# Feed-forward weight tiles in rings with a fourth raw tile, DVE work ordered behind the last emptying, attention steps shifted by one

## The chip, the cores and the metric

The kernel runs on one core of one Trainium2 chip. The metric is the device time of one execution in microseconds (us); the time of a kernel is the median of its runs. The engines are TensorE (PE, with its weight loads PEld), VectorE (DVE), ScalarE (ACT), GpSimd (POOL) and SyncE (SP, which here only issues DMAs).

## The reference

One layer of a streaming encoder on 256 frames of width 2048, in float32. Cut to what matters:

```python
def swiglu(h, w1, w3, w2):
    return (jax.nn.silu(h @ w1) * (h @ w3)) @ w2

x = x + 0.5 * swiglu(rmsnorm(x, ffn1_norm_g), ffn1_w1, ffn1_w3, ffn1_w2)      # inner width 5632
h = rmsnorm(x, mix_norm_g)
qa, ka, va, cq, ckv, k_rope, ga, gb = split(h @ w_in)
y_a = diff_attention_branch(qa, ka, va, ...)       # 8 heads, two softmaxes each, ALiBi
y_b = mla_branch(cq, ckv, k_rope, ...)             # 16 heads, low-rank q and kv, rotary part of 64
merged = sigmoid(ga) * (y_a @ w_branch_a) + sigmoid(gb) * (y_b @ w_branch_b)
x = x + merged @ w_out
x = x + 0.5 * swiglu(rmsnorm(x, ffn2_norm_g), ffn2_w1, ffn2_w3, ffn2_w2)
```

Both attentions read frame s from frame t where s // 64 <= t // 64.

## The kernel before

**Precision.** Every float32 operand is split into a high part (ACT, a cast to fp32r, L120) and a low part (DVE, source less high part, L121); `split` does both. A product is three matmuls: high x high, high x low, low x high.

**Stages in time.** First feed-forward (0 to about 731 us, tiles named f_u and f_d), projection c and differential attention (to about 1090), latent attention (MLA, to about 1460) with the gate and branch products ga and ba of the first branch worked in between, the second branch and w_out (gb, bb, wo, to about 1692), second feed-forward (to the end).

**Feed-forward.** `ffn` walks over 11 groups of 512 inner columns. A group is one `gemm2` (name f_u), which makes the w1 and the w3 half together by Strassen-like sums: its 8 pairs of k-blocks are of kind "S" (seven products, 21 matmuls of 512 columns) or "P" (eight products, 24 matmuls). After groups 2, 5, 8 and 10 two `gemm2` calls (f_d) multiply by w2. That makes 19 `gemm2` calls in each feed-forward. Each uses all accumulators q1 to q7 in PSUM.

For each pair `gemm2` takes a raw tile of 1 MB, which SP loads in two DMAs of 512 KB (L329, L330). For a P pair ACT casts it and DVE subtracts (f_u_hp, f_u_lp). For an S pair DVE first makes sums of the raw quarters (L334, L335, L336), then ACT and DVE split the raw tile (hs, ls) and the sums (hw, lw). After the last pair DVE empties the accumulators: L361 (q5), L370 (q2 and q3), L371 (q4). From the second group on the pairs come in the order UP, whose kinds are S P P S P S P P; so the pair with i = 0 and the one with i = 3 are S.

The result of an f_d product that is not the last is added to x in DRAM by an accumulating DMA from POOL's queue (x_mid, L438).

**Weight tiles.** `wtile` hands out tiles for raw, high and low parts ("raw", "wh", "wl"): it counts modulo 3 while the pool w7 is open (in the feed-forwards) and modulo 2 elsewhere; number 2 lies in w7, numbers 0 and 1 in wp, which is open for the whole kernel. A tile that is handed out again is written when its last reader is done.

**The order of instructions.** The program is written as a stream; a scheduler then fixes, before the run, the order of instructions on each engine and each DMA queue. Every engine runs its own list in order. It may place an instruction of a later tile ahead of one that stands earlier in the source.

**Attention steps.** `later` appends steps to a list, `pend`; each block of a `gemm` (two k-blocks, 12 matmuls) and each pair of a `gemm2` is followed by one step from it; `wait` is an empty step. For two heads of MLA the steps are: `turn(0)` (transposes of the queries, tiles mt, mr, tn, tr), `turn(1)` (of the keys), `weigh` for each head (scores ms, L583; softmax me, L800 to L804), `turn_p` (transposes mp of the weights, L176), `mix` (times v). In one turn of the loop 3 blocks of mq, 2 of mk and 8 of ga or ba run. `branch_out` puts the gate ga through a sigmoid on ACT (L732) after the 8 blocks of ga. The rotary part of the queries is made on POOL (`rotate`, L550 to L552) and doubled by a copy on ACT (L753) before its transposes (mr).

Of the kernel before, what the change touches and what calls it, by code (L numbers as in the profile page):

```python
# [23 lines left out]
F32 = mybir.dt.float32  # L24
# [3 lines left out]
ALU = mybir.AluOpType  # L28
AX = mybir.AxisListType

P = 128
# [22 lines left out]
NW = 512  # L54
KT = 4
# [18 lines left out]
def tile_block(ctx: ExitStack, tc: tile.TileContext, a, out: bass.AP):  # L74
    nc = tc.nc
# [2 lines left out]

    const = ctx.enter_context(tc.tile_pool(name="const", bufs=1))
    big = ctx.enter_context(tc.tile_pool(name="big", bufs=1))  # L80
    pools, turnover = {}, {}
    wp = ctx.enter_context(tc.tile_pool(name="wp", bufs=2))

    def wtile(tag, dt, name):

        i = turnover[tag] = (turnover.get(tag, -1) + 1) % (3 if "w7" in pools else 2)
        if i < 2:
            return wp.tile([P, KT, NW], dt, tag=f"{tag}{i}", bufs=1, name=name)
        return pools["w7"].tile([P, KT, NW], dt, tag=tag, bufs=1, name=name)

    def enter(stack, key, **kw):
        pools[key] = stack.enter_context(tc.tile_pool(name=key, **kw))
        return pools[key]
# [24 lines left out]

    def split(hi, lo, src):
        nc.scalar.copy(out=hi, in_=src)  # L120
        nc.vector.tensor_sub(out=lo, in0=src, in1=hi.bitcast(F32))  # L121

    def split_scaled(hi, lo, src, scale):

# [9 lines left out]
    def later(*steps):  # L134
        pend.extend(steps)
# [43 lines left out]
    def put_transposed(T, kb0, nb, t, src, gain, tmp_pool, name):  # L179

        tp = transposes(lambda i: src[:, i * P:(i + 1) * P], nb, f"tp_{name}")
        sl = slice(t * P, (t + 1) * P)
        f = tmp_pool.tile([P, 4, P], F32, tag="ptf", bufs=1, name=f"f_{name}")
        if gain is None:
            nc.vector.tensor_copy(out=f[:, :nb], in_=tp)
        else:
            nc.vector.tensor_tensor(out=f[:, :nb], in0=tp, in1=gain.unsqueeze(2).to_broadcast([P, nb, P]), op=ALU.mult)
        split(T[:, 0, kb0:kb0 + nb, sl], T[:, 1, kb0:kb0 + nb, sl], f[:, :nb])
# [70 lines left out]
             ("q2", 1, "s", 2), ("q3", 6, "s", 3), ("q4", 3, "w", 2))  # L259
    PLAIN = (("q5", 2, 0), ("q2", 0, 1), ("q3", 4, 0), ("q4", 2, 1))  # L260

    def pair_views(t, n, w):
        return [t[:, i * 2 * w:(i + 1) * 2 * w, :].rearrange("p (h s) k -> p h s k", h=2) for i in range(n)]

# [33 lines left out]
    def gemm2(wleft, wright, pairs, name, due=None, x=None):  # L298
# [13 lines left out]
        def passes(T, prods, in_turn):  # L312


            high = lambda o, s, bh, bl: [(o, T[:, 0, s], bh), (o, T[:, 1, s], bh)]
            low = lambda o, s, bh, bl: [(o, T[:, 0, s], bl)]
            todo = [m for p in prods for f in (high, low) for m in f(*p)] if in_turn else \
                [m for f in (high, low) for p in prods for m in f(*p)]
            for o, x, b in todo:
                left[o] -= 1  # L320
                nc.tensor.matmul(out=q[o], lhsT=x, rhs=b, start=o not in started, stop=left[o] == 0)  # L321
                started.add(o)

        for i in range(n):
            if i == due:
                flush()
            kind, T, k = pairs[i]
            raw = wtile("raw", F32, f"{name}_w")
            nc.sync.dma_start(out=raw[:, 0::3], in_=wright(k))  # L329
            nc.sync.dma_start(out=raw[:, 1:3], in_=wleft(k))  # L330
            h4 = lambda m: (wtile("wh", F32R, f"{name}_h{m}"), wtile("wl", F32R, f"{name}_l{m}"))
            if kind == "S":
                sm = pools["w7"].tile([P, 3, NW], F32, tag="sum", bufs=1, name=f"{name}_s")
                nc.vector.tensor_tensor(out=sm[:, 0:2], in0=raw[:, 0:1].to_broadcast([P, 2, NW]), in1=raw[:, 1::2], op=ALU.add)  # L334
                nc.vector.tensor_add(out=raw[:, 0], in0=sm[:, 0], in1=raw[:, 3])  # L335
                nc.vector.tensor_add(out=sm[:, 2], in0=raw[:, 0], in1=raw[:, 2])  # L336
                sh, sl = h4("s")
                split(sh, sl, raw)
                wh, wl = h4("w")
                split(wh[:, 0:3], wl[:, 0:3], sm)  # L340
                B = {"s": (sh, sl), "w": (wh, wl)}
                for part in (("sw",) if i == 0 else ("s", "w")):
                    passes(T, [(o, slot, B[b][0][:, u], B[b][1][:, u]) for o, slot, b, u in SEVEN if b in part], i == 0)
            else:
                ph, pl = h4("p")
                split(ph, pl, raw)
                units = [(o, slot + j, 1 + j if l else 3 * j) for o, slot, l in PLAIN for j in range(2)]
                passes(T, [(o, slot, ph[:, u], pl[:, u]) for o, slot, u in units], i in (0, n - 1))
            if i == lastS:
                nc.scalar.copy(out=e11, in_=q["q1"])  # L350
                nc.vector.tensor_add(out=e12, in0=q["q6"], in1=e11)
                nc.vector.tensor_add(out=e21, in0=q["q7"], in1=e12)
                if x is not None:
                    (x11, x12), (x21, x22) = ((x[:, t, 0:NW], x[:, t, NW:]) for t in range(NT))
                    nc.vector.tensor_add(out=x11, in0=x11, in1=e11)
                    nc.vector.tensor_add(out=x21, in0=x21, in1=e21)
                    nc.vector.tensor_sub(out=x22, in0=x22, in1=e21)
            if pend:
                pend.pop(0)()
        if x is None:  # L360
            nc.vector.tensor_tensor(out=ev[:, :, NW:], in0=q["q5"].unsqueeze(1).to_broadcast([P, 2, NW]),  # L361
                                    in1=ev.rearrange("p t n -> p (t n)")[:, NW:3 * NW].rearrange("p (a n) -> p a n", a=2),
                                    op=ALU.subtract)
# [4 lines left out]
            nc.vector.tensor_add(out=x12, in0=x12, in1=e12)  # L368
            x1 = x[:, 0]
        nc.vector.tensor_add(out=x1, in0=q23.rearrange("p a n -> p (a n)"), in1=x1)  # L370
        nc.vector.tensor_add(out=x21, in0=q["q4"], in1=x21)  # L371
        return ev


# [67 lines left out]


    f1 = ExitStack()
    enter(f1, "w7", bufs=1)
    enter(f1, "ev", bufs=1)
    enter(f1, "acc", bufs=1, space=bass.MemoryType.PSUM)
    pool = pools["pt"] = f1.enter_context(tc.tile_pool(name="f1", bufs=1))
# [37 lines left out]

    ffn(T, rstd, a["ffn1_w1"][0], a["ffn1_w3"][0], a["ffn1_w2"][0], "D", "C", pool, done1, "f1")
    f1.close()
    del pools["acc"], pools["w7"]
    mixps = ExitStack()  # L490
    enter(mixps, "ps", bufs=2, space=bass.MemoryType.PSUM)
    ptx = ExitStack()
# [10 lines left out]
    with ExitStack() as mixers:  # L503
# [244 lines left out]
        for g in range(MLA_H // 2):  # L748
            qr = mw.tile([P, NT, 2, 2, ROPE], F32, tag="qr", bufs=1, name=f"qr{g}")
            qs, rq = first[0] if g == 0 else q_out(g, q_job(g), qr.rearrange("p t h x e -> p (t h x e)"))  # L750
            for t in range(NT):
                rotate(qr[:, t, :, 0], qs[:, t, :, NOPE:QK_DIM], rtab[0][:, t], [qr[:, t, :, x] for x in range(2)])
            nc.scalar.copy(out=qr[:, :, :, 1], in_=qr[:, :, :, 0])  # L753
            qkT = []

            def turn(i, nope, rope, g=g, qkT=qkT):
# [65 lines left out]
                split(ybT[:, 0, h], ybT[:, 1, h], op[:, 0:S])  # L822

            both = lambda f: [partial(f, hh) for hh in range(2)]
            later(wait, wait, wait, partial(turn, 1, kn, lambda t, w, kh=kh: kh[:, t, w:w + 2]), *both(weigh), wait, *both(turn_p), *both(mix))

            if g + 1 < MLA_H // 2:
                branch_out(g + 1, branch_job(g + 1))
# [37 lines left out]


    with ExitStack() as f2:
        enter(f2, "w7", bufs=1)
        enter(f2, "ev", bufs=1)  # L870
        enter(f2, "acc", bufs=1, space=bass.MemoryType.PSUM)
        pool = pools["pt"] = f2.enter_context(tc.tile_pool(name="f2", bufs=1))

        def done2(x, t, c):
            cs = slice(c * NW, (c + 1) * NW)
            nc.sync.dma_start(out=out_v[:, t, cs], in_=x[:, t, cs])

        ffn(T, rstd, a["ffn2_w1"][0], a["ffn2_w3"][0], a["ffn2_w2"][0], "D", "A", pool, done2, "f2")
        flush()
# [22 lines left out]
```

## Time and profile before

| | us |
|---|---|
| median of 3 runs | 2414.17 (2413.78 to 2415.47) |
| the profiled execution | 2412.0 |
| its span in the profile | 2410.1 |
| PE busy | 2370.2 (98%) |
| DVE busy | 1907.7 (79%) |
| ACT busy | 1256.1 (52%) |
| POOL busy | 127.1 (5%) |

How to read it: PE is busy nearly all the time, but a matmul's end in the profile is modelled, so that matmuls overlap in it and short pauses do not show. The other engines' busy shares are averages over stages that differ. A line of a view of groups reads: source line, engine, operation, written tile <- read tiles, shapes, count | busy us, mean ns | idle us just before, and what ended it. A line of the waits reads: engine, tile and line that waited <- what it waited for: us in total, times, longest. A line of the timeline reads: start us, duration us, engine, line, operation, tiles, count, and in brackets the idle time before it and what ended it. A line of the windows reads: stretch and its length, busy us and instructions of PE, PEld, DVE, ACT and POOL, the clock granted to TensorE (1.00 is full), the busy share of the 16 DMA engines, GB/s. A line of the chain of waits reads: start us, us, engine, tile, line and count of what set the end. A line of the DMA issues reads: tiles, queue, operation, count, KB each, median us from issue to landing.

### The profile page before, as it was taken

What the parts mean: (1) busy time and instruction counts of PE and PEld (TensorE: products, weight loads), DVE (VectorE), ACT (ScalarE), POOL (GpSimd) and SP (SyncE); (2) the same over time, 40 slices, a digit from 0 to 9 for tenths busy, and PEclk for the clock granted to TensorE, in tenths of its full rate; (3) what the DMA queues carried; (4) which work ended last, traced back from release to release, by engine and by line L of the source; (5) the groups of instructions that cost most, each with busy time, mean ns of one, the idle gap of its engine ahead of it and who ended that gap; (6) DMA issues with size and microseconds to landing.
All of it is one profiled execution on the core that took longest, in us unless ns stands there. A gap on an engine that the chain in (4) does not pass through costs nothing.

```text
span 2410.1 us, 29185 instructions
## 1 busy us (share of the span) xinstructions
PE 2370.2 (98%) x10940; PEld 1963.6 (81%) x10940; DVE 1907.7 (79%) x2395; ACT 1256.1 (52%) x1338; POOL 127.1 (5%) x185
## 2 busy tenths in 40 slices
PE   8999999999999999999999999999999999999999
PEld 6788888788788888888888888888788888878777
DVE  8998997988996676767777775556899899789798
ACT  5654554554554455545655644444555455455453
POOL 2000000000000100001121210000000000000000
PEclk9999999999999999999999999999999999999999
DMA  7567667657665545555455456576566766756764
GB/s 263 191 194 235 201 212 205 212 192 210 236 213 181 192 159 175 165 170 173 156 168 171 160 172 208 192 233 208 193 202 209 231 207 192 225 194 203 216 226 158
DMA packets 241918, 476.11 MB, mean 198 GB/s; under 512 B 15156, under 2 KB 28528, under 8 KB 241520
## 3 DMA queue, kind: packets, MB, share of 16 engines
q1 hardware_dynamic: 233280, 446.30, 56.1%
q0 software_dynamic: 7216, 27.29, 5.0%
q8 instruction: 86, 1.41, 0.2%
q10 hardware_dynamic: 1280, 0.66, 0.1%
q14 instruction: 56, 0.46, 0.1%
HBM read 451.12 MB, written 23.07 MB: 197 GB/s over the span
## 4 chain that ended last, share of the span: by engine, by line
PE 82%; DVE 8%; DMA 6%; issue 2%; ACT 1%; SPq 0%; DVEq 0%; ACTq 0%
PE f_u_q L321 29%; PE f_d_q L321 15%; PE da L164 7%; DMA f_u_w<-in_ffn_w 5%; PE ba L164 4%; PE dav L164 4%; PE wo L164 4%; PE bb L164 4%; PE gb L164 3%; PE c L164 2%; PE ga L164 2%; PE mq L164 2%; PE mk L164 2%; DVE f_u_ls L121 2%; DVE f_u_lp L121 2%
## 5 line engine op out<-in xcount | busy, mean ns | idle before, releaser
L120 ACT CAST f_u_hp<-f_u_w 128x2048 fp32r<-128x2048 f32 x110 | 210.1, 1912 | 177.1 <-PE f_u_q L321 101.5
L121 DVE TENSOR_TENSOR f_u_lp<-f_u_w,f_u_hp 128x2048 fp32r<-128x2048 f32 x110 | 250.9, 2285 | 3.7 <-ACT f_u_hp L120 3.7
L321 PE MATMUL f_d_q<-f_d_hp,f_gp 128*128 128x512 f32 x896 | 233.0, 391 | 0.0
L321 PE MATMUL f_u_q<-f_u_hp,hT1p 128*128 128x512 f32 x880 | 225.2, 393 | 0.6 <-ACT f_u_hp L120 0.5
L321 PE MATMUL f_u_q<-f_u_hp,hT2p 128*128 128x512 f32 x880 | 222.9, 390 | 0.2 <-ACT f_u_hp L120 0.2
L120 ACT CAST f_u_hs<-f_u_w 128x2048 fp32r<-128x2048 f32 x66 | 126.2, 1913 | 148.7 <-DVE f_u_w L335 109.4
L321 PEld LDWEIGHTS f_d_q<-f_d_hp,f_gp 128*128 128x128 f32 x896 | 167.3, 188 | 35.3 <-DVE f_gp L121 0.8
L321 PEld LDWEIGHTS f_u_q<-f_u_hp,hT1p 128*128 128x128 f32 x880 | 165.1, 189 | 35.7 <-ACT f_u_hp L120 1.4
L321 PEld LDWEIGHTS f_u_q<-f_u_hp,hT2p 128*128 128x128 f32 x880 | 164.6, 188 | 34.5 <-ACT f_u_hp L120 0.4
L121 DVE TENSOR_TENSOR f_u_ls<-f_u_w,f_u_hs 128x2048 fp32r<-128x2048 f32 x66 | 150.9, 2287 | 24.3 <-ACT f_u_hs L120 24.3
L120 ACT CAST f_d_hp<-f_d_w 128x2048 fp32r<-128x2048 f32 x60 | 113.9, 1913 | 106.2 <-PE f_d_q L321 43.9
L121 DVE TENSOR_TENSOR f_d_lp<-f_d_w,f_d_hp 128x2048 fp32r<-128x2048 f32 x60 | 136.3, 2287 | 23.6 <-ACT f_d_hp L120 23.6
L334 DVE TENSOR_TENSOR f_u_s<-f_u_w 128x1024 f32<-128x1024 f32 x66 | 80.7, 1223 | 72.1 <-DMA f_u_w<-in_ffn_w 72.1
L164 PE MATMUL da<-da_h,hTm 128*128 128x512 f32 x512 | 130.6, 396 | 0.0
L321 PE MATMUL f_d_q<-f_d_lp,f_gp 128*128 128x512 f32 x448 | 128.9, 389 | 0.0
L321 PE MATMUL f_u_q<-f_u_lp,hT2p 128*128 128x512 f32 x440 | 122.7, 391 | 2.1 <-DVE f_u_lp L121 2.0
L321 PE MATMUL f_u_q<-f_u_lp,hT1p 128*128 128x512 f32 x440 | 122.0, 390 | 0.0
L120 ACT CAST f_u_hw<-f_u_s 128x1536 fp32r<-128x1536 f32 x66 | 97.6, 1479 | 42.3 <-DVE f_u_s L336 29.9
L121 DVE TENSOR_TENSOR f_u_lw<-f_u_s,f_u_hw 128x1536 fp32r<-128x1536 f32 x66 | 115.6, 1751 | 0.0
L164 PEld LDWEIGHTS da<-da_h,hTm 128*128 128x128 f32 x512 | 93.4, 188 | 17.9
L321 PEld LDWEIGHTS f_u_q<-f_u_lp,hT2p 128*128 128x128 f32 x440 | 82.5, 188 | 21.0 <-DVE f_u_lp L121 4.0
L121 DVE TENSOR_TENSOR da_l<-da_w,da_h 128x1024 fp32r<-128x1024 f32 x64 | 76.8, 1220 | 28.1 <-ACT da_h L120 28.0
(381 smaller groups left out, 5009.0 us busy)
## 6 DMA issues: line engine op xcount, KB each, us to landing
f_u_w<-in_ffn_w SPq DMA_DIRECT2D x352, 512.0 KB, 4.7
f_d_w<-in_ffn_w SPq DMA_DIRECT2D x176, 512.0 KB, 5.1
da_w<-in_w_in SPq DMA_DIRECT2D x64, 512.0 KB, 4.5
dav_w<-in_w_in SPq DMA_DIRECT2D x32, 512.0 KB, 4.5
ga_w<-in_w_in SPq DMA_DIRECT2D x32, 512.0 KB, 4.6
ba_w<-in_w_branch_a SPq DMA_DIRECT2D x32, 512.0 KB, 4.9
gb_w<-in_w_in SPq DMA_DIRECT2D x32, 512.0 KB, 4.5
bb_w<-in_w_branch_b SPq DMA_DIRECT2D x32, 512.0 KB, 5.0
```

The lines of the kernel that those rows point to most:

```text
L120: nc.scalar.copy(out=hi, in_=src)
L121: nc.vector.tensor_sub(out=lo, in0=src, in1=hi.bitcast(F32))
L164: nc.tensor.matmul(out=po[t][:, :n], lhsT=l, rhs=r_, start=done[t] == 1, stop=done[t] == 3 * len(kbs))
L321: nc.tensor.matmul(out=q[o], lhsT=x, rhs=b, start=o not in started, stop=left[o] == 0)
L334: nc.vector.tensor_tensor(out=sm[:, 0:2], in0=raw[:, 0:1].to_broadcast([P, 2, NW]), in1=raw[:, 1::2], op=ALU.add)
```

## The change

Four things are changed.

1. `wtile` takes tiles from rings, one for each tag, the oldest first. In the feed-forwards the ring of raw tiles has four (two of wp and two of w7, three before), those of high and low parts three as before. `more_weights` adds the tiles of w7 behind the old ones, `fewer_weights` takes them out and keeps the order of the rest.
2. `split` returns its DVE instruction, and the last emptying of a `gemm2` (L371, q4) is noted in `emptied`. For every pair but the first of the next `gemm2`, the pair's first DVE instruction (L334 of an S pair, the low part of a P pair) is ordered behind it. It is an order on DVE's list, with no semaphore.
3. In MLA a `wait` stands ahead of the two `weigh` steps, and both are one step; the number of steps is the same. The copy of the rotary queries goes from ACT to POOL.
4. `put_transposed` uses the tile pf of `put_pairs` while the feed-forward's pools are open, in place of a tile of its own (ptf).

```diff
-    pools, turnover = {}, {}
+    pools = {}
+    rings = {tag: [0, 1] for tag in ("raw", "wh", "wl")}
...
     def wtile(tag, dt, name):
-        i = turnover[tag] = (turnover.get(tag, -1) + 1) % (3 if "w7" in pools else 2)
-        if i < 2:
-            return wp.tile([P, KT, NW], dt, tag=f"{tag}{i}", bufs=1, name=name)
-        return pools["w7"].tile([P, KT, NW], dt, tag=tag, bufs=1, name=name)
+        ring = rings[tag]
+        ring.append(ring.pop(0))
+        i = ring[-1]
+        return (wp if i < 2 else pools["w7"]).tile([P, KT, NW], dt, tag=f"{tag}{i}", bufs=1, name=name)
+
+    def more_weights(stack):
+        enter(stack, "w7", bufs=1)
+        for tag, new in (("raw", (2, 3)), ("wh", (2,)), ("wl", (2,))):
+            rings[tag].extend(new)
+
+    def fewer_weights():
+        del pools["w7"]
+        for ring in rings.values():
+            ring[:] = [i for i in ring if i < 2]
...
     def split(hi, lo, src):
         nc.scalar.copy(out=hi, in_=src)
-        nc.vector.tensor_sub(out=lo, in0=src, in1=hi.bitcast(F32))
+        return nc.vector.tensor_sub(out=lo, in0=src, in1=hi.bitcast(F32))
+
+    def behind(ins, first):
+        tc.add_manual_dep(ins.ins, first.ins.name, mybir.DependencyInfo(mybir.DependencyClass.NoSync, mybir.DependencyReason.DATA),
+                          reason="order")
...
-        f = tmp_pool.tile([P, 4, P], F32, tag="ptf", bufs=1, name=f"f_{name}")
+        if "acc" in pools:
+            f = tmp_pool.tile([P, 2, 7, P], F32, tag="pf", bufs=1, name=f"f_{name}").rearrange("p a s k -> p (a s) k")
+        else:
+            f = tmp_pool.tile([P, 4, P], F32, tag="ptf", bufs=1, name=f"f_{name}")
...
+    emptied = []
...
-                nc.vector.tensor_tensor(out=sm[:, 0:2], in0=raw[:, 0:1].to_broadcast([P, 2, NW]), in1=raw[:, 1::2], op=ALU.add)
+                early = nc.vector.tensor_tensor(out=sm[:, 0:2], in0=raw[:, 0:1].to_broadcast([P, 2, NW]), in1=raw[:, 1::2],
+                                                op=ALU.add)
...
-                split(ph, pl, raw)
+                early = split(ph, pl, raw)
...
+            if i and emptied:
+                behind(early, emptied[-1])
...
-        nc.vector.tensor_add(out=x21, in0=q["q4"], in1=x21)
+        emptied.append(nc.vector.tensor_add(out=x21, in0=q["q4"], in1=x21))
...
-    enter(f1, "w7", bufs=1)
+    more_weights(f1)
...
-    del pools["acc"], pools["w7"]
+    del pools["acc"]
+    fewer_weights()
...
-            nc.scalar.copy(out=qr[:, :, :, 1], in_=qr[:, :, :, 0])
+            nc.gpsimd.tensor_copy(out=qr[:, :, :, 1], in_=qr[:, :, :, 0])
...
-            later(wait, wait, wait, partial(turn, 1, kn, lambda t, w, kh=kh: kh[:, t, w:w + 2]), *both(weigh), wait, *both(turn_p), *both(mix))
+            later(wait, wait, wait, partial(turn, 1, kn, lambda t, w, kh=kh: kh[:, t, w:w + 2]), wait, lambda f=both(weigh): [s() for s in f],
+                  wait, *both(turn_p), *both(mix))
...
-        enter(f2, "w7", bufs=1)
+        more_weights(f2)
```

## The prediction

> **What bounds the kernel.** I read the page's busy times first, then the same by stage (the windows view), then who ended TensorE's idle time (the waits), then the timeline around the longest of those waits.
>
> ```profile
> PE 2370.2 (98%) x10940; PEld 1963.6 (81%) x10940; DVE 1907.7 (79%) x2395; ACT 1256.1 (52%) x1338; POOL 127.1 (5%) x185
> ...
> 1692.00:2405.00 713.00, 704.39 (x3123) 575.95 (x3123) 623.37 (x521) 373.95 (x271) 14.41 (x19) 1.00 0.65 206
> ```
>
> TensorE is the bound everywhere. In the second feed-forward (1692 to 2405) DVE is busy 623.37 of 713 us, 87%, and DMA 0.65: both are close behind. The change touches no matmul, so all that it can win is TensorE's idle time.
>
> A matmul row overstates that TensorE is busy:
>
> ```profile
> L321 PE MATMUL f_d_q<-f_d_hp,f_gp 128*128 128x512 f32 x896 | 233.0, 391 | 0.0
> ...
> 1838.59 47.87 PE f_d_q L321 x210
> ```
>
> A matmul lasts 391 ns, but in the chain 210 of them take 47.87 us, 228 ns apiece. So a wait that shows as x us of idle time costs x + 0.16 us. The waits, by stage: 75 to 731 us (first feed-forward without its filling), 731 to 760, 1090 to 1460, 1692 to 2405:
>
> ```profile
> PE f_u_q L321 <- DVE f_u_e L371: 2.9, 3, 1.2
> PE f_u_q L321 <- DVE f_u_lw L121: 1.0, 1, 1.0
> PE f_u_q L321 <- DVE f_d_e L371: 0.8, 1, 0.8
> ...
> PE c L164 <- DVE f_x L371: 1.9, 1, 1.9
> ...
> PE ms L583 <- DVE tn L126: 3.3, 4, 1.0
> ...
> PE ms L583 <- ACT tn L125: 0.8, 1, 0.8
> PE mp L176 <- DVE me L804: 0.6, 1, 0.6
> ...
> PE f_u_q L321 <- DVE f_u_e L371: 4.2, 4, 1.3
> PE f_u_q L321 <- DVE f_u_lp L121: 2.0, 4, 0.7
> ...
> PE f_u_q L321 <- DVE f_u_lw L121: 1.1, 1, 1.1
> PE f_u_q L321 <- ACT f_u_hs L120: 0.2, 1, 0.2
> PE f_u_q L321 <- ACT f_u_hp L120: 0.2, 1, 0.2
> ```
>
> **A, the order behind the last emptying.** At the end of a feed-forward product L371 empties the last accumulator (q4), and the next product cannot write that bank before. One of the eight L371 waits, on DVE and then on TensorE:
>
> ```profile
> 1928.64 1.23 DVE L370 TENSOR_TENSOR f_u_e<-f_u_q,f_u_e 128x1024 f32<-128x1024 f32 x1
> 1931.04 1.23 DVE L334 TENSOR_TENSOR f_u_s<-f_u_w 128x1024 f32<-128x1024 f32 x1 [1.17 <-DMA f_u_w<-in_ffn_w]
> 1932.18 0.69 DVE L371 TENSOR_TENSOR f_u_e<-f_u_q,f_u_e 128x512 f32<-128x512 f32 x1
> ...
> 1933.38 2.29 DVE L121 TENSOR_TENSOR f_u_lp<-f_u_w,f_u_hp 128x2048 fp32r<-128x2048 f32 x1
> ...
> 1932.92 0.73 PE L321 MATMUL f_u_q<-f_u_hw,hT2s 128*128 128x512 f32 x2 [0.91 <-DVE f_u_e L371]
> ...
> 1937.36 1.52 PE L321 MATMUL f_u_q<-f_u_lp,hT2p 128*128 128x512 f32 x6
> ```
>
> DVE runs in order. A weight sum of the next product (L334) stands ahead of L371 and waits 1.17 us for a load that has not landed, then takes 1.23 us; q4 is ready all that time. The sum belongs to the fourth pair in turn (i = 3), and the change puts the first DVE operation of every pair but the first behind L371. L371 then starts where L370 ends, 1929.87, and ends near 1930.6; TensorE came to need it at 1932.01 (1932.92 less 0.91). The wait goes with 1.4 us to spare. All eight have this shape in the timeline (L370, an idle L334, L371), so A is 2.9 + 0.8 + 4.2 = 7.9 us of idle time in 8 waits: 7.9 + 8 x 0.16 = **9.2 us**. It adds a wait inside DVE only; queued behind it are the sum and the low half f_u_lp, and TensorE waits for those next. Here f_u_lp ends at 1935.67 and its first use came at 1937.36; without the wait that use moves up by 0.91 + 0.16, to 1936.3, still later.
>
> **B, the fourth raw tile.** DVE's idle time ahead of sums, over the run, and the place where it hurts most:
>
> ```profile
> DVE f_u_s L334 <- DMA f_u_w<-in_ffn_w: 72.1, 40, 5.7
> ...
> 2234.52 0.37 SPq L329 DMA_DIRECT2D f_u_w<-in_ffn_w  x1
> ...
> 2245.02 1.23 DVE L334 TENSOR_TENSOR f_u_s<-f_u_w 128x1024 f32<-128x1024 f32 x1 [0.95 <-DMA f_u_w<-in_ffn_w]
> ...
> f_u_w<-in_ffn_w SPq DMA_DIRECT2D x352, 512.0 KB, 4.7
> ...
> x_mid<-f_d_e POOLq DMA_DIRECT2D x12, 1024.0 KB, 9.5
> ```
>
> SP issues a load when a raw tile comes free, and a usual load lands in 4.7 us. The one issued at 2234.52 held DVE until 2245.02, beside the accumulating store x_mid, which itself takes 9.5 us. With four tiles each load is issued one release earlier, here before that store begins. DVE's idle time (13% of this stage) moves ahead of the work, and the late f_u_lw and f_u_lp should go: lw 1.0 and 1.1, lp 2.0 less the 0.7 of term C, 3.4 us in 5 waits, 3.4 + 0.8 = 4.2 us. No row shows four tiles: at worst DVE does no earlier work that TensorE needs (0), at best all 4.2 go. I take half, **2.1 us**, since DVE at 87% stays the next bound and its order is rearranged.
>
> **C, rings.** Entering the second feed-forward, the tile that the old counter picks first is a new one, whose memory is the previous stage's:
>
> ```profile
> 1691.26 1.90 ACT L120 CAST f_u_hp<-f_u_w 128x2048 fp32r<-128x2048 f32 x1 [5.99 <-PE wo L164]
> ```
>
> The cast idles 5.99 us until the last wo product. In the ring the old tiles come first, oldest first, and the second raw load and this cast need not wait. Gone: lp 0.7, hs 0.2, hp 0.2, 1.1 + 3 x 0.16 = **1.6 us** (at worst 0). The 1.9 us wait of c is not touched: no product follows there, so no order is set. The first 75 us fill the pipeline from memory and DVE has no gap there: 0. The shared pf tile in place of ptf has one buffer as before, and its steps come after those of put_pairs: 0, and 0.7 (one 128x512 DVE operation) each for its four uses if they met.
>
> **D, attention steps.** The transposed keys (tn) are made by the step before the scores, with one block of 12 matmuls between:
>
> ```profile
> 1271.62 0.44 PE L583 MATMUL ms<-tn,tn 128*128 128x128 f32 x2 [0.77 <-DVE tn L126]
> ...
> 1276.49 1.28 ACT L732 ACT_TABLE_LOAD   x1
> 1277.79 1.27 ACT L732 ACTIVATE mg<-ga,rstd_n 128x512 f32<-128x512 f32 x2
> 1279.08 1.28 ACT L800 ACT_TABLE_LOAD   x1
> ...
> 1275.76 0.45 PE L583 MATMUL ms<-tn,tn 128*128 128x128 f32 x3
> ...
> 1277.07 4.23 PE mq L164 x24
> ...
> 1283.56 0.54 DVE L804 TENSOR_SCALAR me<-me,msm 128x128 f32<-128x128 f32 x2
> ```
>
> One more block, 12 x 0.228 = 2.7 us, lies between now, more than the longest wait (1.0): the five tn waits go, 3.3 + 0.8 + 5 x 0.16 = **4.9 us**. In exchange the first head's scores come 2.7 us later, just ahead of the second's. Both softmaxes then meet the gate's sigmoid with its table loads, 1.28 + 1.27 + 1.28 = 3.8 us of ACT, which only the second head met before. Late next is mp, the transposes of the weights. The one mp wait (0.6) bounds it: between 0 and 8 iterations x 0.76 = 6.1 us; I take half, **-3.0 us**.
>
> **E, the copy on POOL.** ACT's copy and POOL's nearest operations:
>
> ```profile
> L753 ACT COPY qr<-qr x8: 406/407/407, 1128.7 to 1414.1; 128x256 f32<-128x256 f32 x8
> L550 POOL TENSOR_TENSOR qr<-qs,rtab x32: 456/462/1311, 1125.0 to 1412.1; 128x128 f32<-128x128 f32 x32
> L176 PE MATMUL mr<-ident,qr x32: 272/273/273, 1134.1 to 1419.1; 128*128 128x128 f32 x32
> ```
>
> ACT no longer stands behind POOL's rotation, but TensorE waits for nothing of that. On POOL the copy has twice the elements of L550: between 0.46 and 2 x 1.31 = 2.6 us; I take 0.9. Its reader mr comes 5 us after the copy's start (1128.7 to 1134.1, 1414.1 to 1419.1), so even 2.6 is hidden: 0.
>
> **Sum:** 9.2 + 2.1 + 1.6 + 4.9 - 3.0 = 14.8 us. On the profiled execution, 2412.0 us (its span and 1.9 around it), that gives 2397.2; it ran 2.2 below the median of the three runs, 2414.17, so the forecast is 2414.17 - 14.8 = **2399.4 us**.
>
> **The clock** sets one more bound. After the wait of c:
>
> ```profile
> 728.08:731.49 3.41, 1.49 (x7) 0.96 (x7) 3.41 (x5) 2.82 (x7) 1.22 (x3) 1.00 0.66 162
> 731.49:734.90 3.41, 3.41 (x11) 3.02 (x10) 1.49 (x2) 1.40 (x4) 2.27 (x7) 0.50 1.02 360
> ```
>
> 1.9 us of idle time inside one 3.41 us stretch was followed by one at half clock, 3.41 x 0.5 = 1.7 us lost. If A and B move c against these stretches, the 1.7 may go. The Trainium skill (TensorE: Matmul & The Clock Gate, Part 1) asks for a whole idle window of about 3.4 us; by that rule 1.9 us would cost nothing, and the trace disagrees.
>
> **Rivals.**
>
> 1. *The loads share the engines.* The fourth load finds the 16 DMA engines taken and lands no earlier. For it: the load at 2234.52 next to x_mid. Against it: DMA is busy only 0.65. B and C bring nothing: 9.2 + 4.9 - 3.0 = 11.1, **2403.1**. The Trainium skill (DMA: Bandwidth & Descriptors, Issuing engines are not separate DMA queues) has a rule on this side: DMAs of all issuers run on the same 16 engines and interleave. The trace agrees at that one place.
> 2. *The scores meet the sigmoid.* Between the first head's scores and its mp lie the second head's scores (1275.76 to 1277.07, 1.3 us) and two blocks of mq (24 matmuls, 4.23 us). From the point where its softmax takes more than these 5.5 us, TensorE waits at mp. Before, the head that met the sigmoid took 7.0 us (scores done at 1277.07, weights at 1283.56 + 0.54): 1.5 + 0.16 = 1.7 us a time, 13.3 in 8 iterations. Then 9.2 + 2.1 + 1.6 + 4.9 - 13.3 = 4.5, **2409.7**. Against it: only every second iteration has a sigmoid.
> 3. *The stall moves, the change does not do what it says.* DVE's order is fixed beforehand. If other operations that wait for loads get ahead of urgent ones, the 72.1 us come back elsewhere: **2414**, no change.
> 4. *The order costs more than it frees.* DVE idles at each of the 36 ends of a product that have another after them, waiting for q4's last matmul, and f_u_lp comes late. Price 0.7 + 0.16 = 0.9 each (the longest lp wait), 31 us, less 14.8 won: **2430**. It decides from where f_u_lp slips by more than the 0.6 us left above (1935.67 to 1936.3). For it: DVE at 87%. Against it: its waits for loads give room.
>
> **Chances.** Forecast 0.57, own range 2392 (all of A to D without loss, 19.9, and the 1.7 of the clock) to 2405 (A alone); rival 1 0.13; rival 2 0.08; rival 3 0.12; rival 4 0.10. Differences under 0.2%, 4.8 us, cannot be told from no change. Faster is the forecast and rival 1, with a little of 2: 0.72; within 0.2% the rest of 2 and rival 3: 0.18; slower 0.10. From 2392 to 2413 lie the forecast, rivals 1 and 2 and the near half of 3, about 0.8.
>
> **What would show it.** Right: no TensorE wait on L371 in the feed-forwards; L334 behind L371 everywhere; f_u_lw and f_u_lp waits under 2 us; the cast at 1691 earlier; no ms wait on tn; mp waits of at most 0.8. Wrong: new TensorE waits on f_u_lp just after L371 (rival 4), mp waits of 1.5 us or more (rival 2), or loads still late beside x_mid (rival 1).

## The result, and the profile after

The changed kernel takes 2389.93 us (median, 2389.27 to 2392.05) and the kernel before, run beside it, 2414.82 us (2413.78 to 2416.05): a ratio of 0.9898, 95% interval 0.9881 to 0.9915. That is 24.9 us faster, where 14.8 were forecast, and 2.1 us below the lower end of the range. The direction was right; the size was too small. From profiled execution to profiled execution the difference is 2412.0 - 2389.9 = 22.1 us; the other 2.8 lie between the profiled run of before and its median.

The busy times of the changed kernel, and its second feed-forward in the windows view (columns: window, its length, then the busy time and instruction count of PE, PEld, DVE, ACT and POOL, granted clock, DMA share, GB/s):

```profile
PE 2359.4 (99%) x10940; PEld 1964.8 (82%) x10940; DVE 1913.0 (80%) x2395; ACT 1254.7 (53%) x1330; POOL 129.5 (5%) x193
...
1680.00:2383.00 703.00, 699.99 (x3127) 577.28 (x3125) 623.83 (x521) 373.79 (x270) 15.57 (x19) 1.00 0.65 209
```

TensorE's idle time in the second feed-forward fell from 713 - 704.4 = 8.6 us to 3.0. Here is what ended it, then the same for the start of c and for the latent attention (the waits view, by stage: total us, times, longest):

```profile
PE f_u_q L343 <- DVE x L886: 1.2, 1, 1.2
PE f_d_q L343 <- DVE f_gs L133: 0.8, 1, 0.8
PE f_u_q L343 <- DVE f_u_ls L133: 0.5, 1, 0.5
PE f_u_q L343 <- DVE f_u_lw L133: 0.4, 1, 0.4
...
PE c L181 <- ACT hTm L132: 2.2, 1, 2.2
PE c L181 <- DVE f_x L396: 1.9, 1, 1.9
...
PE mp L193 <- DVE me L830: 2.6, 5, 1.7
PE tp_ya L193 <- DVE f_ya L207: 0.7, 1, 0.7
```

Every wait of TensorE on the last emptying (L371 before, L396 now) is gone but that of c, which the change does not reach; so is every f_u_lp wait and every ms wait on tn. The mp waits have grown from one of 0.6 to five. DVE shows the other side, in the waits view of its own engine and in the timeline at the place that the prediction worked through (columns: start, length, engine, line):

```profile
DVE f_u_e L395 <- PE f_u_q L343: 17.9, 16, 1.1
DVE f_u_s L356 <- DMA f_u_w<-in_ffn_w: 12.4, 12, 1.8
...
1914.91 1.22 DVE L395 TENSOR_TENSOR f_u_e<-f_u_q,f_u_e 128x1024 f32<-128x1024 f32 x1 [1.12 <-PE f_u_q L343]
1916.27 0.69 DVE L396 TENSOR_TENSOR f_u_e<-f_u_q,f_u_e 128x512 f32<-128x512 f32 x1
1916.88 1.22 DVE L356 TENSOR_TENSOR f_u_s<-f_u_w 128x1024 f32<-128x1024 f32 x1
1918.01 2.29 DVE L133 TENSOR_TENSOR f_u_lp<-f_u_w,f_u_hp 128x2048 fp32r<-128x2048 f32 x1
```

DVE now stands for TensorE at the end of a product (17.9 us in 16 waits) and much less for the loads of f_u (72.1 us in 40 waits before, 12.4 in 12 now). For those of f_d it stands more (1.8 us in 2 waits before, 9.2 in 3 now). The sum L356 follows the last emptying at once and finds its load landed.

Where the 22.1 us came from, by the first matmul of each stage in the two traces (the filling up to tp_f; the first feed-forward up to c; c and the differential attention up to mq; the latent attention and both branches up to wo; wo and the second feed-forward):

| | filling | first FFN | c, diff. attention | latent attention | wo, second FFN |
|---|---|---|---|---|---|
| before | 73.9 | 657.2 | 358.6 | 510.5 | 809.9 |
| after | 75.3 | 650.9 | 357.9 | 505.5 | 798.4 |
| gain | -1.4 | 6.3 | 0.7 | 5.0 | 11.5 |
| forecast | 0 | 12.9 for both FFNs | 0 | 1.9 | |

The feed-forwards gave 17.8 instead of 12.9, the attention 5.0 instead of 1.9.

### The profile page after: what moved, and what is told of

Same layout as the page of the kernel before. It is cut to its first block, busy times and chain, and to the rows that moved or that the text cites. A ratio compares the mean times of both kernels' runs of the same rounds, so it can differ in the third digit from the quotient of the medians.

```text
span 2388.1 us, 29197 instructions
## 1 busy us (share of the span) xinstructions
PE 2359.4 (99%) x10940; PEld 1964.8 (82%) x10940; DVE 1913.0 (80%) x2395; ACT 1254.7 (53%) x1330; POOL 129.5 (5%) x193
## 4 chain that ended last, share of the span: by engine, by line
PE 92%; DVE 4%; DMA 2%; issue 1%; ACT 1%; SPq 0%; DVEq 0%; ACTq 0%
PE f_u_q L343 35%; PE f_d_q L343 18%; PE da L181 7%; PE dav L181 4%; PE ba L181 4%; PE wo L181 4%; PE ga L181 4%; PE bb L181 4%; PE gb L181 3%; PE c L181 2%; PE mk L181 2%; PE mq L181 1%; DMA f_d_w<-in_ffn_w 1%; PE tp_f L193 1%; PE ms L609 1%
## 5 line engine op out<-in xcount | busy, mean ns | idle before, releaser
L181 PEld LDWEIGHTS da<-da_h,hTm 128*128 128x128 f32 x512 | 93.4, 188 | 17.9
L343 PEld LDWEIGHTS f_d_q<-f_d_lp,f_gp 128*128 128x128 f32 x448 | 83.9, 188 | 18.5 <-DVE f_d_lp L133 1.1
L343 PEld LDWEIGHTS f_u_q<-f_u_lp,hT1p 128*128 128x128 f32 x440 | 83.1, 189 | 17.4
```

Of the source, the lines that this page charges most:

```text
L181: nc.tensor.matmul(out=po[t][:, :n], lhsT=l, rhs=r_, start=done[t] == 1, stop=done[t] == 3 * len(kbs))
```

## The experiments

These ran on three chips: e1 to e4, e13 and e14 on one, e5 to e8 on a second, e9 to e12 on a third. The kernel before takes 2409.36 us (median of 21 runs, 2406.72 to 2413.42) and 2409.23 on the first of them, 2408.89 on the second and 2409.86 on the third. The record does not name the chip of the result above, which is called the first set here. Each difference below is against the set that the run belongs to, and the stage lengths are cut as in the table above; each comes from one profiled execution.

**The order alone (e1_fence).** The kernel before with the order only:

```diff
-                split(ph, pl, raw)
+                early = split(ph, pl, raw)
...
+            if i and emptied:
+                behind(early, emptied[-1])
...
-        nc.vector.tensor_add(out=x21, in0=q["q4"], in1=x21)
+        emptied.append(nc.vector.tensor_add(out=x21, in0=q["q4"], in1=x21))
```

> Before, with only the order behind the last emptying added. Theory (the terms add, each with its own waits): the eight TensorE waits on L371 go and nothing else changes, 9.2 us less than before, 2405. Rival (the fence alone clears the DVE stall that makes later tiles late): the f_u_lp and f_u_lw waits go too, 13 us or more. Second rival (DVE idles at the fence): 5 us or less, with new waits on f_u_lp.

Measured: 2400.42 us, ratio 0.9966 (0.9953 to 0.9978), 8.9 us faster (5.3 to 11.3 by the interval). The feed-forwards' waits on the last emptying are gone, and no new f_u_lp wait has come. Term A, 9.2, lies inside the interval. The waits that were priced are not quite the same on these chips: the kernels below that keep the feed-forward of before (e3_mla, e8_shift, e14_copy) show six to eight of them, 6.2 to 7.0 us, which is 7.2 to 8.3 by the prediction's price.

**Rings and the fourth raw tile, without the order (e2_raw4).**

```diff
+        for tag, new in (("raw", (2, 3)), ("wh", (2,)), ("wl", (2,))):
+            rings[tag].extend(new)
```

> Before, with only the rings, the fourth raw tile and the shared pf tile. Theory (terms add): B whole and C, 5.8 us, and the pauses too short for the profile's idle time, about 3 us: 9 us less, 2406, with the L371 waits still there. Rival (the earlier loads also end the DVE idle time in front of L371): the L371 waits go without any fence, 15 us or more, and A and B are two ways to the same gain.

Measured: 2413.79 us, ratio 1.0021 (1.0011 to 1.003), 4.4 us slower, where the theory had 9 faster and its rival 15. The trace shows the place: in DVE's timeline, TensorE's timeline, then two windows of the columns above.

```profile
659.66 1.23 DVE L384 TENSOR_TENSOR f_u_e<-f_u_q,f_u_e 128x1024 f32<-128x1024 f32 x1 [1.11 <-PE f_u_q L335]
666.39 1.23 DVE L348 TENSOR_TENSOR f_d_s<-f_d_w 128x1024 f32<-128x1024 f32 x1 [5.51 <-DMA f_d_w<-in_ffn_w]
667.53 0.68 DVE L385 TENSOR_TENSOR f_u_e<-f_u_q,f_u_e 128x512 f32<-128x512 f32 x1
...
668.27 0.74 PE L335 MATMUL f_d_q<-f_d_hw,f_gp 128*128 128x512 f32 x2 [3.21 <-DVE f_u_e L385]
...
666.15:669.56 3.41, 1.29 (x6) 1.05 (x6) 3.17 (x4) 1.31 (x2) 0.00 (x0) 1.00 0.02 5
669.56:672.97 3.41, 3.41 (x10) 2.64 (x9) 3.41 (x5) 3.01 (x2) 0.00 (x0) 0.50 0.17 31
```

With four tiles DVE's order, fixed beforehand, has a sum of the next product (L348) ahead of the last emptying (L385); it stands 5.51 us for its load, and TensorE 3.21. The next 3.41 us run at a granted clock of 0.50. The old stall is longer at such places: two waits on L385 take 6.8 us, the longest 3.6, where the longest in the feed-forwards of before took 1.3. The trace has four half-clock stretches between the filling and the end, that of before one. Three more at 1.7 us apiece would be 5.1 us, an estimate about as large as the whole loss.

**The attention steps, with the copy on POOL (e3_mla) and without it (e8_shift).**

```diff
-            ...both(weigh), wait, *both(turn_p), *both(mix))
+            ...wait, lambda f=both(weigh): [s() for s in f],
+                  wait, *both(turn_p), *both(mix))
...
-            nc.scalar.copy(out=qr[:, :, :, 1], in_=qr[:, :, :, 0])
+            nc.gpsimd.tensor_copy(out=qr[:, :, :, 1], in_=qr[:, :, :, 0])
```

> Before, with only the shifted attention steps and the copy on POOL. Theory: the MLA stage gets shorter by 4.8 us as in the changed kernel, 2410. Rival (the stage gains only because the feed-forward change shifted its start and the clock stretches): 1 to 2 us.

> Before, with only the shift of the attention steps; the copy stays on ACT. Theory (the tn waits are the gain, and the clock that stays whole with them): all of the attention part, 7 to 9 us less than before. Rival (ACT, no longer stopped behind POOL's rotation, brings half): 3 to 5 us.

Measured: e3_mla 2400.97 us, ratio 0.9968 (0.9956 to 0.9981), 8.4 us faster; e8_shift 2403.27, ratio 0.9979 (0.9969 to 0.9989), 5.6 faster. The theory's 4.8 for e3_mla lies inside its interval (4.6 to 10.6); e8_shift falls between its theory (7 to 9) and its rival (3 to 5), and its interval (2.6 to 7.5) settles neither. The latent attention takes 504.9 us in the first and 506.2 in the second; it took 510.5 in the profile of before, and 510.6 to 512.6 in the six other traces with the old steps and the old copy. The tn waits are gone in both, and what is left in e3_mla are five mp waits and one of the stage's end:

```profile
PE mp L176 <- DVE me L804: 1.9, 5, 1.0
PE tp_ya L176 <- DVE f_ya L187: 0.8, 1, 0.8
```

**The copy alone (e14_copy).**

> The kernel before with the copy of the rotated queries on POOL alone, nothing else. The forecast's step E: 0, within 1.5 us of before, since its reader comes 5 us later. Rival: ACT's queue no longer stands behind POOL's rotation and short pauses of TensorE go: 1.5 to 3 us faster (the attention steps with the copy were 2.8 us ahead of the attention steps alone, at the edge of what those runs could tell).

Measured: 2406.08 us, ratio 0.999 (0.9981 to 0.9998), 3.1 us faster by the medians, 0.5 to 4.6 by the interval; the latent attention takes 508.0, 2.5 less than in the profile of before, and 2.6 to 4.6 less than in the six others. Step E had put this at 0, and the rival is nearer. The rows show what it missed: first e14's waits in the stage, then ACT's timeline in the kernel before, then in e14.

```profile
PE ms L583 <- DVE tn L126: 1.2, 2, 1.0
...
PE mp L176 <- DVE me L804: 0.6, 1, 0.6
```

```profile
1169.69 0.41 ACT L753 COPY qr<-qr 128x256 f32<-128x256 f32 x1 [4.59 <-DVE u_mq L114]
1170.00 1.04 ACT L120 CAST ga_h<-ga_w 128x1024 fp32r<-128x1024 f32 x1
...
1186.72 1.77 ACT L120 CAST mq_h<-mq_w 128x768 fp32r<-128x768 f32 x2 [5.48 <-DMA mq_w<-in_mla_w_qb]
1188.40 0.58 ACT L125 ACTIVATE tn<-mt 128x512 fp32r<-128x512 f32 x1
```

```profile
1169.11 1.05 ACT L120 CAST ga_h<-ga_w 128x1024 fp32r<-128x1024 f32 x1 [1.55 <-PE mk L164]
...
1188.45 1.78 ACT L120 CAST mq_h<-mq_w 128x768 fp32r<-128x768 f32 x2 [4.76 <-PE mt L176]
```

ACT stood 4.59 us at the copy, with a weight cast (ga_h, the eleventh of the 32) behind it. Sixteen microseconds later it stands 5.48 us for the load of mq_w, and the cast that makes tn is behind that. The trace of e14 runs 2.5 us later here (its first mq is at 1092.17 in place of 1089.68). Counted from that mq, the eleventh ga_h cast starts 3.4 us earlier in e14, and mq_h 0.8 us earlier and no longer behind a load; the ms wait there falls from 0.78 to 0.17 us. Over the stage ACT's waits for mq_w fall from 24.6 us in 5 to 13.8 in 3, and the ms waits of tn from 4.1 us (3.3 + 0.8) to 1.2. That the early cast frees the tile for the load of mq_w is read from the order of these rows and not tried by itself.

**Rings with three raw tiles (e4_ring3).** As e2_raw4, with `("raw", (2,))`.

> Before, with the rings, oldest tile first, but still three raw tiles. Theory: only the entry of the second feed-forward changes, 1.6 us less, 2413, not to be told from no change by the time, but the cast of f_u_hp at the entry starts earlier and the three entry waits are gone from the trace. Rival (the rings do most of what the fourth tile was credited with): 5 us or more.

Measured: 2408.44 us, ratio 0.9995 (0.9986 to 1.0004): no difference that can be told, and term C's 1.6 lies inside the interval. At the entry of the second feed-forward the cast no longer waits, and the three waits named are gone. The fourth tile, then, and not the ring, made e2_raw4 slower.

**The feed-forward parts together (e5_ffn); the whole change with three raw tiles (e6_three) and with four (e7_whole).**

```diff
-        for tag, new in (("raw", (2, 3)), ("wh", (2,)), ("wl", (2,))):
+        for tag, new in (("raw", (2,)), ("wh", (2,)), ("wl", (2,))):
```

(that is e6_three against the changed kernel; e5_ffn has the changed kernel's feed-forward with the old attention steps and copy).

> The changed kernel with the old attention steps and the copy on ACT: fence, rings and fourth raw tile. Theory (the fourth tile pays only behind the fence: alone it let weight sums get ahead of the emptying and cost 4.4 us, with the fence it brings the loads early and nothing gets ahead): 15 to 17 us less than before, more than the fence alone (8.9) by 6 or more. Rival (parts add as they were measured one by one, -8.9 + 4.4): 4 to 5 us less.

> The changed kernel with three raw tiles in the ring in place of four (a third of w7, no fourth). Theory: the fourth tile is worth 6 us or more behind the fence, so this is 17 to 19 us less than before, with DVE idle in front of the sums (L334) for tens of us. Rival (the gain beyond the fence and the steps comes from the rings' order): 23 us or more less, like the whole change.

> The changed kernel itself, beside its parts on one chip. Theory: 23 to 26 us less than before, and the sum of the feed-forward part (fence, rings, fourth tile) and of the attention part (8.4). Rival (before was slow on the other chip, where its DMAs landed later): 18 us or less.

Measured: e5_ffn 2397.92, ratio 0.9954 (0.9941 to 0.9966), 11.0 us faster; e6_three 2392.97, ratio 0.9931 (0.9918 to 0.9945), 15.9 faster; e7_whole 2391.6, ratio 0.9927 (0.9915 to 0.994), 17.3 faster. All three gains fall short of their theories (15 to 17, 17 to 19, 23 to 26); e7_whole falls where its rival had it, at 18 or less. Two things follow. The fourth tile behind the order is worth 1.4 (e7 less e6) to 2.1 (e5 less e1), which these intervals cannot tell from nothing; the loss of e2_raw4 is gone. By stages e7_whole has 2.5 us less than e6_three in the last stage (799.1 and 801.6) and 2.0 more in the first feed-forward (654.3 and 652.3), where the place shown next costs it 2.77 us of waiting and a stretch at half clock. And the changed kernel is nearly the same in the first set and here (2389.93 and 2391.6), while the kernel before is not (2414.82 and about 2409 on all three chips): the first result holds some 5.5 us that belong to that set's kernel before. Here the interval of the gain, 14.5 to 20.5 us, reaches down to the forecast's 14.8.

In e7_whole one place is left where a later pair's sum stands ahead of an earlier pair's low half (DVE's timeline, TensorE's, then windows):

```profile
664.05 1.22 DVE L356 TENSOR_TENSOR f_d_s<-f_d_w 128x1024 f32<-128x1024 f32 x1 [6.94 <-DMA f_d_w<-in_ffn_w]
665.20 2.28 DVE L133 TENSOR_TENSOR f_d_lp<-f_d_w,f_d_hp 128x2048 fp32r<-128x2048 f32 x1
...
667.53 1.00 PE L343 MATMUL f_d_q<-f_d_lp,f_gp 128*128 128x512 f32 x2 [2.77 <-DVE f_d_lp L133]
...
664.60:668.00 3.40, 0.63 (x3) 0.39 (x3) 3.40 (x3) 0.00 (x0) 0.00 (x0) 0.97 0.00 0
668.00:671.41 3.41, 3.41 (x12) 2.63 (x11) 3.41 (x4) 1.85 (x1) 0.00 (x0) 0.53 0.76 218
```

The order covers the last emptying only, not this.

**Late loads made on purpose (e9_before_load, e10_whole_load, e11_three_load, e13_raw4_load).** Were late loads what sets the first set's kernel before apart? Each kernel gets extra copies that nobody reads:

```diff
+            nc.sync.dma_start(out=spare[len(spared)], in_=wright(k)[:, 0])
+            spared.append(i)
             nc.sync.dma_start(out=raw[:, 0::3], in_=wright(k))
```

> The kernel before, and ahead of every pair's two raw loads one more transfer on SP's queue: 256 KB of the same weights are copied from memory to a scratch array in memory that nobody reads (176 copies, a quarter more than the raw loads' own bytes). Theory L (the kernel before waits where loads land late: its gain from the change depends on when they land, and differs from chip to chip by it): this kernel grows by 6 to 40 us over before, and its waits on f_u_e, f_u_lp and f_d_lp grow. Rival M (the difference between chips is not one of loads): it grows by under 3 us, or by as much as the changed kernel with the same copies.

> The changed kernel with the same 176 copies. Theory L: the order and the fourth raw tile together take the loads' landing off TensorE's path, so this grows by at most a third of what the kernel before grows by. Rival M: both grow by the same, within 2 us.

> The changed kernel with three raw tiles in place of four, and the same 176 copies. If the fourth raw tile is what makes late loads harmless: it grows by at least 3 us more than the changed kernel with four tiles does. If the order alone does it: by the same, within 2 us (without copies the fourth tile was worth 1.4 us).

> The kernel before with rings and the fourth raw tile, without the order, and the same extra copies (they all run in the first feed-forward: DMA there 0.90). The copies cost the first feed-forward 29.0 us in the kernel before, 32.2 with the order and three raw tiles, 6.5 with the order and four. Theory F (the fourth raw tile by itself makes late loads harmless): they cost this kernel under 10 us over its own 2413.8 without copies, so under 2424. Rival O (a sum that waits for a late load must also stand behind the last emptying, or TensorE waits for it): 15 to 35 us, 2429 to 2449, with long waits on f_u_e and f_d_e.

There are 264 copies, not the 176 of the expectations (the down products have pairs too), and the traces show all of them between 2.6 and 584 us, none in the second feed-forward, since nothing held them back. So the stage to compare is the first feed-forward:

| | order | raw tiles | time | first FFN, plain | with copies | growth |
|---|---|---|---|---|---|---|
| e9_before_load | no | 3 | 2439.94 | 657.2 (before) | 686.2 | 29.0 |
| e11_three_load | yes | 3 | 2426.1 | 652.3 (e6_three) | 684.5 | 32.2 |
| e13_raw4_load | no | 4 | 2422.87 | 660.2 (e2_raw4) | 666.4 | 6.2 |
| e10_whole_load | yes | 4 | 2398.55 | 654.3 (e7_whole) | 660.8 | 6.5 |

The plain stages and those with copies come from different chips, one execution each. The medians of whole runs grow alike: 30.1, 33.1, 9.1 and 7.0 us. With the copies the raw loads of this stage land after 6.2 to 6.7 us on average, without them after 5.0 to 5.3. Ratios to before: 1.0126 (1.0112 to 1.014), 1.0068 (1.0055 to 1.008), 1.006 (1.0046 to 1.0074) and 0.9957 (0.9945 to 0.997). The stage in three of them, by windows and DVE's waits: e9_before_load, e11_three_load, e10_whole_load.

```profile
76.00:761.00 685.00, 660.43 (x2905) 533.50 (x2903) 577.08 (x487) 350.44 (x263) 11.53 (x15) 1.00 0.88 290
...
DVE f_u_s L336 <- DMA f_u_w<-in_ffn_w: 48.7, 22, 7.9
```

```profile
76.00:760.00 684.00, 661.92 (x2905) 537.04 (x2904) 577.97 (x488) 351.07 (x264) 11.52 (x15) 0.99 0.88 291
...
DVE f_u_s L358 <- DMA f_u_w<-in_ffn_w: 45.8, 23, 8.3
```

```profile
77.00:736.00 659.00, 650.18 (x2901) 533.94 (x2899) 576.98 (x486) 350.37 (x263) 11.52 (x15) 1.00 0.90 301
...
DVE f_u_s L358 <- DMA f_u_w<-in_ffn_w: 28.4, 11, 6.7
```

At a DMA share of 0.9 in place of 0.65, TensorE is idle 24.6 us (685 less 660.43) and 22.1 us with three tiles, 8.8 with four and the order, and 12.4 with four alone. The order makes little difference to the growth: with it or without it, three tiles lose about 30 us and four about 6. The part of theory L that late loads cost the kernel before time holds, and so does theory F (the fourth tile by itself takes most of that away); that the order does it falls, and e11_three_load decides it. That late loads set the first set apart is the other part of theory L, and these runs do not show it.

**The waits that are left (e12_best).** Against the changed kernel:

```diff
-            split(wh, wl, raw)
+            early = split(wh, wl, raw)
+            if emptied:
+                behind(early, emptied[-1])
...
-            later(wait, wait, wait, partial(turn, 1, kn, ...), wait, lambda f=both(weigh): [s() for s in f],
-                  wait, *both(turn_p), *both(mix))
+            later(wait, wait, partial(turn, 1, kn, ...), wait, lambda f=both(weigh): [s() for s in f],
+                  wait, wait, *both(turn_p), *both(mix))
```

> The changed kernel with the same order for c's two low halves (behind the last emptying as well) and, in the latent attention, the second transposition and the scores one block of matmuls earlier, the transposition of the weights where it was. If the waits that are left in the changed kernel are what they look like: 1.2 of c's 1.9 us on f_x go (two low halves of 1.09 us stand ahead of the emptying), and 3.4 us of the five mp waits (2.6 + 5 x 0.16): 4.6 us under the changed kernel. Rival: the keys are not ready a block earlier (they need the reciprocal root on POOL and two DVE operations behind it), so TensorE waits at mt in place of mp: 0 to 1.2 us under it, or above it.

Measured: 2388.84 us, ratio 0.9914 (0.9899 to 0.9929); e7_whole, in another set, had 0.9927, so the 2.8 us between them, where 4.6 were expected, are not settled by these intervals. In the trace both edits do what they say. The latent attention takes 503.0 in place of 504.9, so 1.9 of the 3.4 expected, and its waits are

```profile
PE tp_ya L195 <- DVE f_ya L209: 1.1, 1, 1.1
PE mo L847 <- ACT mpT L132: 0.5, 2, 0.3
```

with no mp wait and none at mt. c's wait on f_x is gone too; in its place c stands 0.9 for its weights' cast, and its stage is no shorter (357.9, 357.7 in e7_whole).

## Why the prediction was right and where it failed

**What bounds the kernel: right, but not all of it was counted.** TensorE's pauses are where the gain came from, stage by stage. Those that the waits view lists are only a part of them (below).

**A, the order: right.** 9.2 forecast, 8.9 measured alone, and the eight waits are gone. No new f_u_lp wait came just behind, as rival 4 needed. That the two numbers are so close is in part luck: on that chip the priced waits were 7.2 to 8.3, and short pauses went with them.

**Short pauses: the step that failed.** The sum priced only what the waits view lists. A matmul row overlaps the next by 0.16 us, and the view lists no idle time under 0.15 us, so a pause of less than about 0.3 us has no row there. The sum put such pauses at nothing without a reason. They can be worked out from the starts of all matmuls: where the interval to the next start is longer than the usual one (the median over all traces for the same two kinds of matmul), the rest is a pause. In us, from the two profiled executions of the first set:

| | before | after | fell by | forecast |
|---|---|---|---|---|
| both feed-forwards (with wo), pauses over 0.3 | 17.0 | 4.8 | 12.2 | 12.9 |
| the same, 0.02 to 0.3 | 10.9 | 6.3 | 4.6 | 0 |
| latent attention and branches, over 0.3 | 6.7 | 4.3 | 2.4 | 1.9 |
| the same, 0.02 to 0.3 | 10.2 | 7.7 | 2.4 | 0 |

The long pauses, which are those that the view lists, gave 14.6 us, where 14.8 were forecast. That this is so close is in part luck, since B and the give-back in D were each taken at half of a bound. The short ones gave 7.0 more, and that is nearly all of the 7.3 by which the two executions differ beyond the forecast. By the semaphores that had just been set, the short pauses come from the same engine as the long ones. In the feed-forwards those behind an emptying (L370, L371) fell from 3.0 us to none and those behind DVE's other results from 2.9 to 1.2; in the attention those behind DVE fell from 3.9 to 1.5. What the others moved is 0.5 or less. So the mechanism was right (DVE comes late and TensorE waits), and the sum had too few of its waits. This is a count in one trace of each kernel; no experiment took the short pauses away alone.

**B, the fourth raw tile: right as a term, wrong about the tile by itself.** Behind the order it gives 1.4 to 2.1 where loads land in time, near the 2.1 forecast. The prediction's bounds, 0 to 4.2, do not hold without the order: alone the tile costs 4.4 us. With DMA at 0.9 it gives 23.7 us of the first feed-forward behind the order (684.5 less 660.8). The forecast saw that it is late loads that hold DVE (72.1 us in 40 waits), but priced the tile by the few that reached TensorE in one execution.

**The kernel before in the first set: open.** The other 2.8 us of the 24.9 lie between the median of before and its profiled execution. The four runs of before in that set (2413.78 or more) lie some 5 us above the medians of the three chips. The kernels e3_mla, e8_shift and e14_copy keep the feed-forward of before, with the same order of work on DVE, ACT and TensorE. Their last stage (wo and the second feed-forward) takes 804.5, 805.9 and 804.0 us, where before takes 809.9. TensorE's waits of that feed-forward in e3_mla:

```profile
PE f_u_q L321 <- DVE f_u_e L371: 2.2, 2, 1.2
PE f_u_q L321 <- DVE f_u_lp L121: 1.2, 2, 0.7
PE tp_o L176 <- DVE x L859: 1.2, 1, 1.2
PE f_u_q L321 <- DVE f_u_lw L121: 0.5, 1, 0.5
PE f_u_q L321 <- ACT f_u_hp L120: 0.2, 1, 0.2
```

They sum to 5.3 us, where before has 9.1. Late loads would be a cause, since the copies show that this kernel turns them into time. But the mean time from issue to landing of the 264 loads of that stage is 5.03 us in all three and 5.11 in before, and the first feed-forward speaks against it: there the mean is 5.19 in before and 5.11 to 5.13 in the three, and the stage is no longer (657.2, and 657.5 to 658.2). What made the last stage 4 to 6 us longer is not shown.

**C, rings: not to be told apart.** 1.6 forecast, 0.9 measured with an interval from -1.0 to 3.4. The waits that it named are gone, and the cast at the entry no longer waits.

**D, the attention steps: right in mechanism.** The tn waits (4.9) went, and mp waits came in their place: 2.6 + 5 x 0.16 = 3.4 us after, 0.76 before, a give-back of 2.6 where 3.0 was put. But one of the five is 1.7 long, above the 0.8 that was said to be the sign of being right and above the 1.5 said for rival 2; rival 2's 13.3 us did not come. Alone the shift shortens its stage by 4.3 us or more (e8_shift), where 1.9 was put: the listed waits went as forecast there too, and the rest is in shorter pauses.

**E, the copy: wrong, the second step that failed.** "TensorE waits for nothing of that" followed the copy's own reader (5 us later) and not what is queued behind the copy on ACT. Alone it gave 2.5 us in the stage, against the profile of before. Both D and E take away tn waits, so they overlap there: by stages 2.5 and 4.3 (e8_shift) alone, 5.6 together. The run times (3.1, 5.6 and 8.4 us) are too coarse to show it. Behind the shift the copy is worth 1.3 us (506.2 less 504.9), so it is the smaller of the two misses.

**The clock: the stretch went, its 1.7 us hardly.** The changed kernel shows no half-clock stretch between its filling and its end in the first set, and two in e7_whole, at 668 and behind the wait of c at 729. But at c TensorE, no longer slowed, waits longer for hTm. That wait was

```profile
PE c L164 <- ACT hTm L120: 0.9, 1, 0.9
```

in the kernel before and is 2.2 us after. The stage from c on is 0.7 us shorter than before, and e7_whole, with the stretch, takes 357.7 us there against 357.9 without it. So the bound of 1.7 was too large at this place.

The rivals: loads do land later beside other traffic (6.2 to 6.7 us with the copies), as rival 1 said, and there the tile pays rather than brings nothing. Rival 3 (waiting work gets ahead elsewhere) is true of the tile without the order, and of the place at 664 us.

## What to carry to other kernels

A view of waits has a least length. Before a forecast takes a list of waits for all that can be won, work out from the starts of the bounding engine's instructions what the pauses below that length sum to, and which engine ends them: here 21 us before, of which 7 went.

A deeper buffer and a fixed order of work are one decision: the buffer alone lets waiting work get ahead of urgent work (4.4 us slower), the order alone leaves late loads harmful (32 us under heavy traffic), together they did neither but for one place. Price a buffer by how the kernel takes late loads, with traffic added on purpose, and not by the stalls of one execution. When an instruction leaves an engine's queue, look at what stood behind it there, not only at who reads its result.

## What the runs showed of the hardware

- A granted clock of 0.50 for one stretch of 3.41 us followed idle time that was far less than a whole stretch: 2.1 us of 3.41 (PE 1.29) in e2_raw4 above, and 1.5 us (PE 1.91) at another place of the same trace:

```profile
362.37:365.78 3.41, 1.91 (x8) 1.16 (x8) 3.17 (x3) 0.00 (x0) 0.00 (x0) 1.00 0.86 272
365.78:369.19 3.41, 3.41 (x10) 2.64 (x9) 0.00 (x0) 0.00 (x0) 0.00 (x0) 0.50 0.77 277
```

  The same wait of c that was followed by one in the kernel before (1.92 us idle in its stretch) was followed by none in the changed kernel in the first set. The stretches come every 3.413 us; counted on from the end of the half clock at the start (17.98 us), this is the one that holds the wait, and the next:

```profile
724.53:727.94 3.41, 1.67 (x8) 1.60 (x9) 3.41 (x4) 3.35 (x8) 1.61 (x3) 1.00 0.92 237
727.94:731.35 3.41, 3.41 (x20) 3.14 (x20) 0.87 (x2) 0.94 (x4) 2.08 (x8) 1.00 1.04 366
```

  It holds 1.74 us of idle time. With all stretches of all sixteen traces cut in this way after the filling, each with 1.88 us or more at full clock was followed by half clock. Of those with 1.5 to 1.83 us three were (1.51 here, 1.51 in e13_raw4_load at 2047.41, 1.60 in e9_before_load at 1466.24) and the others were not, the largest 1.83 (e14_copy at 729.25). So from about 1.9 us on a stretch was always followed by half clock here, and below that the idle time alone does not decide; what does is open. Where a border falls matters, since it splits a pause. The Trainium skill (TensorE: Matmul & The Clock Gate, Part 1) asks for a whole idle window; these rows differ, and the measurement decides.
- The same kernel before takes 2414.8 us in the first set and 2408.9 to 2409.9 on three chips later, 0.2% apart, while the changed kernel is within 0.1% in two sets. Whether it is the chip or the occasion, these runs do not show. A gain measured in one set holds something of that set.
